# The forget gate's cumulated sums, read from DRAM into all partitions and added by VectorE with the mask, in place of a fourth score product on TensorE

## The chip, the core and the metric

The kernel runs on one core of one Trainium2 chip. A core has TensorE (PE in the profile; PEld is its loading of weights), VectorE (DVE), ScalarE (ACT), GpSimd (POOL) and SyncE (SP), each with its own instruction queue worked in order, and 16 DMA engines that all queues share. Nearly all transfers here are issued from SP. The metric is the device time of one execution in microseconds; the kernel before takes 613.34 us (median of three runs, 612.76 to 614.09).

## The reference

A decoder block over 528 tokens (16 learned ones and 512 real ones), model width 1024, float32. From `u = rmsnorm(h)` one wide projection gives the inputs of two attentions with 16 heads each, and all gates. The MLA branch ("latent" below) has rotary scores of its own; the forgetting attention (FoX, "forget" below) adds differences of cumulated log forget gates to its scores:

```python
log_f = jax.nn.log_sigmoid((f_logit + fox_forget_b[l]).astype(jnp.float32)).transpose(0, 2, 1)
cum = jnp.cumsum(log_f, axis=-1)
...
s = jnp.einsum('bhqd,bhkd->bhqk', qb, k, preferred_element_type=jnp.float32) * scale
if cq is not None:
    s = s + (cq[..., :, None] - cum[:, :, None, :])
s = jnp.where(key_pos[None, :] <= qpos[:, None], s, -jnp.inf)
p = jax.nn.softmax(s, axis=-1)
return jnp.einsum('bhqk,bhkd->bhqd', p.astype(v.dtype), v)
```

The two branch outputs are gated, projected, summed, projected again and normalized onto the residual stream. In a softmax over keys the term `cq` of the query is the same for a whole row and falls out, so the kernel adds only `-cum` of the key.

## The kernel before

Weights and activations are split into a high and a low part, and a product is made of three matmuls (high by high, high by low, low by high). ScalarE casts the high part of a weight tile (`wh`, L142), GpSimd or VectorE subtracts for the low one (`wl`, L118).

**Order of the work.** An opening normalizes the tokens, makes the small projections and the gate's sums; its instruction order is written by hand in three lists (`OPENING`, `MIDDLE`, `LAST`) for all engines. Then come 16 attention passes, two heads each: for each pair of heads 0 to 7 first the forget pass (`br` = 1), then the latent pass (`br` = 0). From the second pass on, TensorE's order is the program's, and a scheduler places the other engines' and SP's instructions by priority and by what they depend on. A last part mixes the branches and projects out.

**A pass** (`attention`): the scores of query blocks 0, 1 and 2 (group 0) fill four PSUM banks (`st`, a pool of four), two for each head; then the value products of the pass before (`values`, tile `ov`); then query block 3 (group 1) fills the four banks again, in two pieces of 272 and 256 keys; then projections of later passes. Both heads' matmuls use 64 rows of the array each and run side by side. For every piece one VectorE instruction (L915) adds the mask, scales, writes `sf` to SBUF and keeps the running minimum `nb`. ScalarE takes the exponential of `sf` with its sum, VectorE inverts the sum (`su`, `ri`), ScalarE and VectorE write the high and low halves of the weights (`pn`, L953 and L954), and eight DMA transposes on SP (L961) turn them into `pt`, which the value products in the next pass read.

**The fourth product.** In a forget pass `sets` gives three products of query and key and a fourth: `ONE`, whose first two rows of each half are ones, by `CT`, which holds the high and low part of `-cum/scale` in those rows. `CT` is filled by `chc` and `chl` for pair 0, and by `load_ct` (L288) from `c_dram` for later pairs. A latent pass has two rotary products in that place. `maskt` (bfloat16) is zero except for one block of 128 columns with -1e30 above the diagonal; a slice of it serves every piece.

`gT[0]` and `gT[1]` hold the gated outputs of the two branches, one slot of 512 columns for a pair of heads; the slots are empty until their pair's value products, and the rotary work of the opening and of the latent pass of pair 1 (`pe_unit`) borrows some of them.

## Time and profile before

| | us |
|---|---|
| profiled execution, its own time | 612.84 |
| its span, first to last instruction | 611.0 |
| median of three runs | 613.34 |
| VectorE busy | 384.7 |
| ScalarE busy | 385.2 |
| GpSimd busy | 174.3 |
| matmuls into `st`, forget and latent, three products of query and key (480) | 47.2 |
| VectorE, score pieces with mask (128) | 48.5 |

Busy times are sums of instruction durations on one engine; matmuls are pipelined, so theirs overlap one another. TensorE's granted clock is full over the whole span (mean 0.999). The DMA engines moved 84.63 MB, and their packets took 53.4% of 16 engines' time.

### The profile page before, as it was taken

What the parts mean: (1) busy time and instruction counts of PE and PEld (TensorE: products, weight loads), DVE (VectorE), ACT (ScalarE), POOL (GpSimd) and SP (SyncE); (2) the same over time, 40 slices, a digit from 0 to 9 for tenths busy, and PEclk for the clock granted to TensorE, in tenths of its full rate; (3) what the DMA queues carried; (4) which work ended last, traced back from release to release, by engine and by line L of the source; (5) the groups of instructions that cost most, each with busy time, mean ns of one, the idle gap of its engine ahead of it and who ended that gap; (6) DMA issues with size and microseconds to landing.
All of it is one profiled execution on the core that took longest, in us unless ns stands there. A gap on an engine that the chain in (4) does not pass through costs nothing.

```text
span 611.0 us, 11593 instructions
## 1 busy us (share of the span) xinstructions
PE 602.2 (99%) x4066; PEld 493.3 (81%) x4066; DVE 384.7 (63%) x1026; ACT 385.2 (63%) x839; POOL 174.3 (29%) x231
## 2 busy tenths in 40 slices
PE   9999999999999999999999999999999999999995
PEld 5889779889889889889888898878888865565885
DVE  5949664774774774773675665668877765646133
ACT  6856884874874884784785766768667743534421
POOL 2002562436543444253343532500000000004600
PEclk9999999999999999999999999999999999999999
DMA  9613577768577477567556665758341146342202
GB/s 301 137 35 109 151 144 182 150 166 206 135 173 183 99 162 156 133 151 167 133 132 159 143 144 145 171 119 240 99 144 36 35 122 228 97 135 77 99 34 105
DMA packets 204556, 84.63 MB, mean 138 GB/s; under 512 B 122757, under 2 KB 197893, under 8 KB 204498
## 3 DMA queue, kind: packets, MB, share of 16 engines
q1 hardware_dynamic: 204496, 83.89, 53.4%
q8 instruction: 32, 0.52, 0.4%
q14 instruction: 26, 0.21, 0.1%
q10 hardware_dynamic: 2, 0.00, 0.0%
HBM read 54.43 MB, written 4.00 MB: 96 GB/s over the span
## 4 chain that ended last, share of the span: by engine, by line
PE 88%; DMA 3%; DVE 2%; issue 2%; ACT 2%; POOL 1%; SPq 0%; DVEq 0%; POOLq 0%; ACTq 0%
PE pg L92 14%; PE z L92 13%; PE st L92 8%; PE v L92 8%; PE po L92 7%; PE fq L92 7%; PE fk L92 7%; PE py L92 6%; PE ov L92 5%; PE yx L92 3%; PE psm L92 2%; PE yy L92 2%; PE mq L92 2%; PE vt L95 1%; DMA ht<-in_x_dram 1%
## 5 line engine op out<-in xcount | busy, mean ns | idle before, releaser
L118 POOL TENSOR_TENSOR wl<-wraw,wh 128x1024 fp32r<-128x1024 f32 (+1 forms) x54 | 119.5, 2218 | 256.1 <-ACT wh L142 246.5
L142 ACT CAST wh<-wraw 128x1024 fp32r<-128x1024 f32 (+1 forms) x74 | 72.9, 986 | 81.2 <-issue 34.4
L925 ACT ACTIVATE sf<-sf,nb 128x144 f32<-128x144 f32 (+3 forms) x128 | 71.9, 566 | 2.8 <-DVE nb L915 2.8
L953 ACT ACTIVATE pn<-sf,ri 128x128 f16<-128x128 f32 (+3 forms) x128 | 61.9, 552 | 16.3 <-ACT sf L925 14.4
L954 DVE SCALAR_TENSOR_TENSOR pn<-sf,ri,pn 128x128 f16<-128x128 f32 (+3 forms) x128 | 66.2, 558 | 8.4 <-ACT pn L953 8.4
L92 PE MATMUL pg<-uTh,wh 128*128 128x512 f32 x128 | 51.9, 406 | 0.0
L915 DVE CUSTOM_DVE_ANT_0 sf<-st,maskt 128x272 f32<-128x272 f32 (+2 forms) x128 | 48.5, 435 | 4.4 <-PE st L92 4.4
L92 PE MATMUL z<-uTh,wh 128*128 128x512 f32 x128 | 51.1, 399 | 0.0
L92 PE MATMUL z<-uTh,wl 128*128 128x512 f32 x128 | 50.1, 391 | 0.0
L92 PE MATMUL z<-uTl,wh 128*128 128x512 f32 x128 | 50.1, 391 | 0.0
L92 PE MATMUL pg<-uTh,wl 128*128 128x512 f32 x128 | 50.0, 391 | 0.0
L92 PE MATMUL pg<-uTl,wh 128*128 128x512 f32 x128 | 49.9, 389 | 0.0
L92 PE MATMUL st<-hlk,hlq 64*128 64x272 f32 (+3 forms) x480 | 47.2, 306 | 0.0
L92 PE MATMUL py<-g,yw 128*128 128x512 f16 x192 | 42.6, 379 | 0.6 <-DVE yw L1239 0.6
L92 PEld LDWEIGHTS st<-hlk,hlq 64*128 64x128 f32 x480 | 35.0, 185 | 5.9 <-ACT wh L142 2.9
L92 PE MATMUL fk<-uTh,wh 128*128 128x256 f32 (+1 forms) x128 | 36.6, 286 | 0.0
L92 PE MATMUL v<-uTh,wh 128*128 128x256 f32 (+1 forms) x128 | 36.5, 285 | 0.0
L92 PE MATMUL fk<-uTl,wh 128*128 128x256 f32 (+1 forms) x128 | 36.5, 285 | 0.0
L92 PE MATMUL fk<-uTh,wl 128*128 128x256 f32 (+1 forms) x128 | 36.5, 285 | 0.0
L92 PE MATMUL v<-uTl,wh 128*128 128x256 f32 (+1 forms) x128 | 36.4, 285 | 0.0
L92 PE MATMUL v<-uTh,wl 128*128 128x256 f32 (+1 forms) x128 | 36.4, 285 | 0.0
L92 PEld LDWEIGHTS <-yw 128*128 128x128 f16 x192 | 17.9, 98 | 22.7 <-DVE yw L1239 1.1
(301 smaller groups left out, 1494.2 us busy)
## 6 DMA issues: line engine op xcount, KB each, us to landing
wraw<-in_w_in_dram SPq DMA_DIRECT2D x56, 512.0 KB
yraw<-in_w_br_fox_dram SPq DMA_DIRECT2D x8, 512.0 KB
yraw<-in_w_br_mla_dram SPq DMA_DIRECT2D x8, 512.0 KB
wraw<-in_w_out_dram SPq DMA_DIRECT2D x8, 512.0 KB
pt<-pn SPq DMA_TRANSPOSE x128
xr<-in_x_dram SPq DMA_DIRECT2D x4, 512.0 KB
out_dram<-yo SPq DMA_DIRECT2D x8, 256.0 KB
QP<-qpe_dram SPq DMA_DIRECT2D x7, 256.0 KB
```

The lines of the kernel that those rows point to most:

```text
L92: nc.tensor.matmul(*a, **k)
L95: nc.tensor.transpose(*a)
L118: eng.tensor_tensor(out=lo, in0=src, in1=f32(hi), op=ALU.subtract)
L142: nc.scalar.copy(wh[:, :n], raw[:, :n])
L915: nc.vector.tensor_tensor_reduce(out=sf_of(h, b)[:, c0 : c0 + w], in0=ps[h][:, o : o + w], in1=maskt[:, m0 : m0 + w], scale=-scale, scalar ...
L925: nc.scalar.activation(sf, sf, AF.Exp, bias=sums["nb"][:, h, b : b + 1], scale=-1.0, accum_out=sums["su"][:, h, b : b + 1])
L953: nc.scalar.activation(hi, sf, AF.Copy, scale=rib)
L954: nc.vector.scalar_tensor_tensor(out=lo, in0=sf, scalar=rib, in1=hi, op0=ALU.mult, op1=ALU.subtract)
```

## The change

The fourth product goes. `c_dram` keeps `-cum/scale` in float32 (no split), one row for each head. For a pair of heads, four DMAs read the two heads' rows into all 128 partitions: `load_diag` puts the whole row of 528 into `cdiag`, `load_off` puts the first 400 into the last slot of `gT[0]` and `gT[1]`. The mask's triangle is added to the four diagonal blocks of `cdiag` in one instruction over 128 x 1024 (`mask_diag`), by VectorE for pair 0 and by GpSimd for the others. The VectorE instruction that empties a score piece then takes its addend from one of these tiles in place of `maskt`; where a piece holds keys both before and in the diagonal block, it becomes two instructions. To make room, `junk` moves and some borrowed slots of `gT` are others; the second half of the rotary table for `pe_unit(1)` is loaded by a DMA of its own.

```diff
-    CT = fx.tile([128, L], F32R, tag="CT", name="CT")
-    ONE = fx.tile([128, 128], F32R, tag="ONE", name="ONE")
...
+    cdiag = fx.tile([128, 2, L], F32, tag="cdiag", name="cdiag")
...
-    def load_ct(pr):
+    OFF = META + 384
+
+    def load_diag(pr):
         for h in range(2):
-            nc.sync.dma_start(f32(CT[64 * h : 64 * h + 2, :]), c_dram[:, 2 * pr + h, :])
+            nc.sync.dma_start(cdiag[:, h], c_dram[2 * pr + h : 2 * pr + h + 1, :].broadcast_to([128, L]))
+
+    def load_off(pr):
+        for h in range(2):
+            nc.sync.dma_start(gT[h][:, KD - 1, 0:OFF],
+                              c_dram[2 * pr + h : 2 * pr + h + 1, 0:OFF].broadcast_to([128, OFF]))
+
+    def mask_diag(eng):
+        d = cdiag[:, :, META:].rearrange("p h (b c) -> p h b c", b=4)
+        m = maskt[:, 400:L].unsqueeze(1).unsqueeze(1).broadcast_to([128, 2, 4, 128])
+        eng.tensor_tensor(out=d, in0=d, in1=m, op=ALU.add)
...
             if pr > 1 and i:
-                load_ct(pr)
+                load_diag(pr)
+                load_off(pr)
+                mask_diag(nc.gpsimd)
...
     def chc():
-        nc.scalar.activation(ch[:, 0], fa[:, 0], AF.Copy, scale=-1.0 / SC_FOX)
-        for h in range(2):
-            nc.sync.dma_start(f32(CT[64 * h : 64 * h + 1, :]), f32(ch[h : h + 1, 0]))
+        nc.scalar.activation(ch, fa[:, 0], AF.Copy, scale=-1.0 / SC_FOX)
+        nc.sync.dma_start(c_dram, ch)
 
     def chl():
-        nc.vector.scalar_tensor_tensor(out=ch[:, 1], in0=fa[:, 0], scalar=-1.0 / SC_FOX, in1=f32(ch[:, 0]),
-                                       op0=ALU.mult, op1=ALU.subtract)
...
+        load_diag(0)
...
     LAST = (
-        "r1 r0 wlm pg2 pg3 pg4 pg5 pg6 pg7 th whb Lf"
+        "Lo bt r1 r0 wlm pg2 pg3 pg4 pg5 pg6 pg7 th whb Lf"
     ).split()
...
             def srcs():
-                nc.sync.dma_start(rp, rope_pe)
+                for cs in range(2):
+                    nc.sync.dma_start(rp[cs], rope_pe[:, cs])
...
                 if br:
-                    return out + [(ONE[hs], CT[hs, ks])]
+                    return out
...
+            def terms(h, b, c0, w):
+                if not br:
+                    m0 = 384 - 128 * b + c0
+                    return [(c0, w, maskt[:, m0 : m0 + w])]
+                d, e = META + 128 * b if b else 0, c0 + w
+                out = [(c0, min(d, e) - c0, gT[h][:, KD - 1, c0 : min(d, e)])] if c0 < d else []
+                return out + ([(d, e - d, cdiag[:, h, d:e])] if e > d else [])
...
-                                    mm(ps[h][:, o : o + w], Q, K, start=(i == 0), stop=(i == 4 - br))
+                                    mm(ps[h][:, o : o + w], Q, K, start=(i == 0), stop=(i == 4 - 2 * br))
...
+                                for c1, n, add in terms(h, b, c0, w):
+                                    with tc.high_priority(offset=100):
+                                        nc.vector.tensor_tensor_reduce(
+                                            out=sf_of(h, b)[:, c1 : c1 + n], in0=ps[h][:, o + c1 - c0 : o + c1 - c0 + n],
+                                            in1=add, scale=-scale, scalar=3.0e38 if c1 == 0 else nb,
+                                            op0=ALU.add, op1=ALU.min, accum_out=nb)
...
-                    load_ct(1)
+                    load_diag(1)
+                    load_off(1)
```

`Lo` in `LAST` is `load_off(0)`, `bt` is `mask_diag` on VectorE; for pair 1 `mask_diag` on GpSimd stands at the end of the first pass.

The change moves instructions on VectorE and on SP. The first place is VectorE in the forget pass of pair 4: the score pieces of group 0 (`sf_3251`; `st_3252` and `st_3253` are the two heads' first banks, `st_3274` and `st_3275` their second), and what stands behind them. Each piece is followed by a row that writes out `nb`, left out here but for the first. Before:

```order
L915 ISA sf_3251,nb_3248<-st_3252,maskt 128x144
L915 ISA nb_3248 128x1
...
L915 ISA sf_3251,nb_3248<-st_3252,maskt 128x272
...
L915 ISA sf_3251,nb_3248<-st_3253,maskt 128x144
...
L915 ISA sf_3251,nb_3248<-st_3253,maskt 128x272
...
L915 ISA sf_3251,nb_3248<-st_3274,maskt 128x400
...
L915 ISA sf_3251,nb_3248<-st_3275,maskt 128x400
...
L934 TENSOR_SCALAR su_3249<-su_3249 128x2x3
L935 RECIPROCAL ri_3250<-su_3249 128x2x3
L976 SCALAR_TENSOR_TENSOR gT_831<-ov_3292,vsc_2897,sil_2918 128x512
```

The same place in the changed kernel, where `gT_822` and `gT_826` are the two tiles `gT`, `st_3263` and `st_3264` the second banks, and `sf_3309` group 1:

```order
L927 ISA sf_3242,nb_3239<-st_3243,gT_822 128x144
...
L927 ISA sf_3242,nb_3239<-st_3244,cdiag 128x144
...
L927 ISA sf_3242,nb_3239<-st_3243,cdiag,nb_3239 128x128
...
L927 ISA sf_3242,nb_3239<-st_3264,gT_826 128x272
...
L927 ISA sf_3242,nb_3239<-st_3263,cdiag,nb_3239 128x128
L927 ISA nb_3239 128x1
L988 SCALAR_TENSOR_TENSOR gT_822<-ov_3281,vsc_2885,sil_2906 128x512
...
L927 ISA sf_3309,nb_3239<-st_3310,gT_822 128x272
...
L927 ISA sf_3309,nb_3239<-st_3321,cdiag,nb_3239 128x128
...
L946 TENSOR_SCALAR su_3240<-su_3240 128x2x3
```

Group 0 has ten pieces where it had six, group 1 six where it had four, and `su`, `ri` and with them `pn` now stand behind all sixteen instead of between the groups.

The second place is SP in the same pass, with its transposes (`pt_...` is the tile of one head). Before:

```order
L133 DMA wraw_2859<-in_w_in_dram 128x8x128
L961 DMA_TRANSPOSE pt_629<-pn_627 128x3x128
L288 DMA CT<-c_dram 2x528
L961 DMA_TRANSPOSE pt_630<-pn_627 128x3x128
L288 DMA CT<-c_dram 2x528
L961 DMA_TRANSPOSE pt_629<-pn_627 128x5x128
```

And in the changed kernel:

```order
L132 DMA wraw_2847<-in_w_in_dram 128x8x128
L289 DMA gT_822<-c_dram 128x400
L289 DMA gT_826<-c_dram 128x400
L285 DMA cdiag<-c_dram 128x528 x2
L973 DMA_TRANSPOSE pt_624<-pn_622 128x3x128
L973 DMA_TRANSPOSE pt_625<-pn_622 128x3x128
```

The loads for the next pair stand ahead of all eight transposes; they wait until VectorE has read the tiles for the last time in this pass.

The third place is SP from the end of the first forget pass to the transposes of the latent pass of pair 0. Before:

```order
L961 DMA_TRANSPOSE pt_630<-pn_628 128x9x128
L288 DMA CT<-c_dram 2x528 x2
L781 DMA qpe_dram<-gT_831 6x16x512 x4
...
L961 DMA_TRANSPOSE pt_629<-pn_627 128x7x128
L961 DMA_TRANSPOSE pt_630<-pn_627 128x7x128
L961 DMA_TRANSPOSE pt_629<-pn_628 128x9x128
```

And in the changed kernel:

```order
L973 DMA_TRANSPOSE pt_625<-pn_623 128x9x128
L285 DMA cdiag<-c_dram 128x528 x2
L289 DMA gT_822<-c_dram 128x400
L289 DMA gT_826<-c_dram 128x400
L786 DMA qpe_dram<-gT_822 6x16x512 x4
...
L973 DMA_TRANSPOSE pt_625<-pn_622 128x7x128
L751 DMA gT_822<-in_rope_pe_dram 128x512
L973 DMA_TRANSPOSE pt_624<-pn_623 128x9x128
```

Four broadcast loads stand where two small ones did, and the second half of the rotary table is loaded between the transposes, since its slot of `gT[0]` is free only after the stores to `qpe_dram`.

More of the change, by code (lines that the diff above doesn't have):

```diff
@@ L80, in block_kernel @@
     nc.gpsimd.memset(ALL1, 1.0)
-    junk = const.tile([128, 1024], BF16, tag="junk", name="junk")
     padp = ctx.enter_context(tc.tile_pool(name="padp", bufs=1, side="right"))
     padp.tile([128, 56], F32, tag="pad", name="pad")
-    c_dram = dram.tile([2, NH, L], F32, tag="cdram", name="c_dram")
+    c_dram = dram.tile([NH, L], F32, tag="cdram", name="c_dram")
     qpe_dram = dram.tile([NH, 2, 2, 16, S], F32, tag="qpedram", name="qpe_dram")
@@ L95, in tps, with sumsq @@
         nc.tensor.transpose(*a)
-    def sumsq(src, acc):
+    def sumsq(src, acc, junk):
         with nc.allow_low_precision(reason="a bound for a power of two"):
@@ L396, in chc @@
     def chc():
-        nc.scalar.activation(ch[:, 0], fa[:, 0], AF.Copy, scale=-1.0 / SC_FOX)
-        for h in range(2):
-            nc.sync.dma_start(f32(CT[64 * h : 64 * h + 1, :]), f32(ch[h : h + 1, 0]))
+        nc.scalar.activation(ch, fa[:, 0], AF.Copy, scale=-1.0 / SC_FOX)
+        nc.sync.dma_start(c_dram, ch)
     def chl():
-        nc.vector.scalar_tensor_tensor(out=ch[:, 1], in0=fa[:, 0], scalar=-1.0 / SC_FOX, in1=f32(ch[:, 0]),
-                                       op0=ALU.mult, op1=ALU.subtract)
-        for h in range(2):
-            nc.sync.dma_start(f32(CT[64 * h + 1 : 64 * h + 2, :]), f32(ch[h : h + 1, 1]))
-        for i in range(2):
-            nc.sync.dma_start(c_dram[i], f32(ch[:, i]))
+        load_diag(0)
     later.update(ab=ab, ex=ex, lnf=lnf, st=st_, scan=scan, chc=chc, chl=chl)
@@ L732, in pe_unit @@
         def pe_unit(g, get0=None, put=None):
-            tt, rp = (gT[1][:, 2:6], gT[1][:, 6:8]) if g else (tt0, rope0_t)
+            tt = gT[1][:, 2:6] if g else tt0
+            rp = (gT[1][:, 6], gT[0][:, 2]) if g else [rope0_t[:, i] for i in range(2)]
             def rr(*sl):
-                return gT[0][:, 4 * g : 4 * g + 4].bitcast(F32R)[sl]
+                return gT[0][:, 3 * g : 3 * g + 4].bitcast(F32R)[sl]
             out = []
@@ L1041, in block_kernel @@
                 [128, KD, S], F32, tag=f"gT{b}", name=f"gT{b}") for b in range(2)]
-            later.update(r1=lambda: rope0[1](1), r0=lambda: rope0[1](0), Lf=fills[1][0][1].load)
+            later.update(r1=lambda: rope0[1](1), r0=lambda: rope0[1](0), Lf=fills[1][0][1].load,
+                         Lo=lambda: load_off(0), bt=lambda: mask_diag(nc.vector))
             for name in LAST:
@@ L1115, in block_kernel @@
         s1x = ExitStack()
+        junk = scp.tile([128, 1024], BF16, tag="junk", name="junk", bufs=1)
         aop = s1x.enter_context(tc.tile_pool(name="aop", bufs=4))
@@ L1225, in square @@
             def square(self, _):
-                sumsq(self.raw, self.ss[:, 0:1])
+                sumsq(self.raw, self.ss[:, 0:1], junk)
             def scale(self):
```

21 lines of the change are left out of this document (7 added, 14 removed).

## The prediction, written before the run

> **What bounds the kernel now.** I read the page first, then what TensorE waited for, then the chain of waits.
>
> ```profile
> span 611.0 us, 11593 instructions
> PE 602.2 (99%) x4066; PEld 493.3 (81%) x4066; DVE 384.7 (63%) x1026; ACT 385.2 (63%) x839; POOL 174.3 (29%) x231
> PE 88%; DMA 3%; DVE 2%; issue 2%; ACT 2%; POOL 1%; SPq 0%; DVEq 0%; POOLq 0%; ACTq 0%
> ```
>
> TensorE runs for 99% of the span and makes up 88% of the chain that ended last; the other engines sit at 63% or less. The second view says whether TensorE ever waits inside the attention (engine, line, what it waited for, us in total, times, longest):
>
> ```profile
> PE v L92 <- DVE hlk L118: 0.4, 1, 0.4
> PE ov L92 <- DMA pt<-pn: 0.3, 1, 0.3
> ```
>
> Only 0.7 us, both early. So a TensorE instruction that goes is time that goes, and whatever makes TensorE wait anew is time that comes. The two questions are what the fourth product costs on TensorE, and whether its replacement stays hidden. The chain of waits shows one forget pass (pair 4) and the latent pass behind it (start us, us, what):
>
> ```profile
> 240.33 1.88 PE st L92 x24
> 242.21 1.97 PE ov L92 x26
> 244.18 1.17 PE st L92 x16
> ...
> 260.11 2.29 PE st L92 x29
> ...
> 264.37 1.42 PE st L92 x13
> ```
>
> A pass is two groups of scores with the previous pass's value products (`ov`) between them. The forget pass has four products, the latent pass five of the same widths.
>
> **What goes: the fourth product.**
>
> ```profile
> L92 PE MATMUL st<-CT,ONE x80: 269/282/343, 64.8 to 375.3; 64*128 64x272 f32 x32, 64*128 64x144 f32 x16, 64*128 64x400 f32 x16, 64*128 64x256 f32 x16
> ```
>
> All 80 go. Their own durations overlap (both heads run side by side), so I take the difference of the passes: one product costs 2.29 - 1.88 = 0.41 us in the first group and 1.42 - 1.17 = 0.25 us in the second. That is 0.66 us a pass and **-5.28 us** over eight. Two small DMA issues a pass, VectorE's `chl` and the memsets of `CT` and `ONE` go as well; TensorE waits for none of them, so they count nothing.
>
> **What VectorE gets.** VectorE empties the score banks of pair 4 like this (start us, us, instruction):
>
> ```profile
> 241.61 0.31 DVE L915 CUSTOM_DVE_ANT_0 sf<-st,maskt 128x144 f32<-128x144 f32 x1
> 241.84 0.44 DVE L915 CUSTOM_DVE_ANT_0 sf<-st,maskt 128x272 f32<-128x272 f32 x1
> ...
> 242.79 0.57 DVE L915 CUSTOM_DVE_ANT_0 sf<-st,maskt 128x400 f32<-128x400 f32 x1
> 243.29 0.57 DVE L915 CUSTOM_DVE_ANT_0 sf<-st,maskt 128x400 f32<-128x400 f32 x1
> ...
> 245.87 0.71 DVE L976 SCALAR_TENSOR_TENSOR gT<-ov,vsc,sil 128x512 f32<-128x512 f32 x1
> ...
> 247.83 0.47 DVE L915 CUSTOM_DVE_ANT_0 sf<-st,maskt,nb 128x256 f32<-128x256 f32 x1
> 248.24 0.47 DVE L915 CUSTOM_DVE_ANT_0 sf<-st,maskt,nb 128x256 f32<-128x256 f32 x1
> 248.64 1.93 DVE L954 SCALAR_TENSOR_TENSOR pn<-sf,ri,pn 128x256 f16<-128x256 f32 x4
> ```
>
> From start to start, 144 columns take 0.23, 272 take 0.36, 400 take 0.50, and 256 with the running minimum `nb` as input 0.41. The slope is 0.27/256 us a column, so a piece of 128 with `nb` takes about 0.41 - 0.13 = 0.28. Before, the first group is 2 x (0.23 + 0.36 + 0.50) = 2.18 us; after, 2 x (0.23 + 0.23 + 0.28 + 0.36 + 0.28) = 2.76 us. That the added operand is now float32 rather than bfloat16 isn't shown for this instruction; the row at 248.64 reads float32 from SBUF alone at 0.46 us for 256 columns, close to the 0.41 here, so I take no extra cost. The upper bound, double time per column, is a rival below.
>
> The banks matter because there are four, and the second group needs all of them again (TensorE, start us, us):
>
> ```profile
> 244.11 0.64 PE L92 MATMUL st<-hlk,hlq 64*128 64x272 f32 x6
> 244.58 0.29 PE L92 MATMUL st<-CT,ONE 64*128 64x272 f32 x2
> 244.71 0.51 PE L92 MATMUL st<-hlk,hlq 64*128 64x256 f32 x6
> ...
> 262.33 0.41 PE L92 MATMUL ov<-pt,vm 80*64 80x512 f16 x2
> ```
>
> The second group's second bank starts at 244.71. Without the product it would start 0.41 + 0.13 earlier, at 244.17. VectorE, starting at 241.61 as before (the `v` scale ahead of it is unchanged), ends at 241.61 + 2.76 + 0.08 (an instruction's end lies that far behind the next one's start) = 244.45. Before it ended at 243.86, 0.85 us in time; now it is **0.28 us late**. Pairs 2 to 7 have the same offsets within 0.02 us: **+1.7 us**. Pair 0 has projections between its groups and pair 1 is late for another reason, so both are left out. Bounds: 0, if the first evacuations overlap better, to 0.6 a pass.
>
> [...]
>
> **The transposes.** The order moves VectorE's `su`, `ri` and `pn` behind all score pieces, and SP's four broadcast loads ahead of the eight transposes, where two small loads lay among them.
>
> ```profile
> 247.41 1.18 SPq L961 DMA_TRANSPOSE pt<-pn  x1
> 248.69 0.39 SPq L288 DMA_DIRECT2D CT<-c_dram  x1
> ...
> 250.93 8.01 SPq L961 DMA_TRANSPOSE pt<-pn  x6
> ```
>
> ```profile
> 248.45 0.72 ACT L925 ACTIVATE sf<-sf,nb 128x528 f32<-128x528 f32 x1
> ```
>
> After: score pieces of group one end at 244.37, `gT` takes 0.62 to the next start, group two 2 x (0.36 + 0.28 + 0.28) = 1.84, so 246.83; two exponentials of 0.72 to 248.3; the first `pn` pair about 0.4 on each engine, so the first transpose starts near 249.1 and not at 247.41. The loads wait for group two's last read of their tiles (246.8 at most) and take four issues of some 0.43 (the row at 45.82 below, also 128 rows): done at 248.5, just hidden. The eight transposes need 258.94 - 247.41 less two `CT` loads with gaps of 0.48, 10.6 us: they end at 259.7, the last one issued at 258.4. TensorE wants it at 262.33 - 0.66 + 0.28 = 261.95, 3.6 us later. How long does one take to land?
>
> ```profile
> 81.84 4.11 DMA pt<-pn
> ```
>
> ```profile
> 397.75 10.65 SPq L961 DMA_TRANSPOSE pt<-pn  x8
> ```
>
> ```profile
> 409.00:409.50 0.50, 0.50 (x4) 0.41 (x3) 0.50 (x1) 0.27 (x1) 0.00 (x0) 1.00 1.05 232
> 409.50:410.00 0.50, 0.50 (x4) 0.40 (x3) 0.50 (x1) 0.00 (x0) 0.00 (x0) 1.00 0.00 0
> ```
>
> Once, in the opening, 4.11 us. At the end of attention, with no load behind it, the last issue began at 408.40 - 1.33 = 407.07 and the DMA engines (last two columns: share, GB/s) fell silent by 409.5: 2.4 us. Inside the passes I take 2.4 to 3.3: **0** here, with a margin of 0.3 to 1.2 us.
>
> In the opening there is no margin:
>
> ```profile
> 83.26 0.76 SPq L288 DMA_DIRECT2D CT<-c_dram  x2
> 84.08 3.91 SPq L781 DMA_DIRECT2D qpe_dram<-gT  x4
> ...
> 95.05 3.15 SPq L961 DMA_TRANSPOSE pt<-pn  x2
> ...
> 98.91 8.73 SPq L961 DMA_TRANSPOSE pt<-pn  x6
> ```
>
> ```profile
> 45.82 0.43 SPq L746 DMA_DIRECT2D gT<-in_rope_pe_dram  x1
> ```
>
> ```profile
> 109.16 0.51 PE L92 MATMUL ov<-pt,vm 80*64 80x512 f16 x2
> ```
>
> SP is busy without a gap from 83.26 to 107.64, and the last transpose, issued at 107.64 - 1.46 = 106.18, is wanted at 109.16. After, four loads of 0.43 with gaps of 0.09 replace 0.76 (+1.3), and half of the `rope_pe` load now lies among the transposes (+0.4): issued at 107.9, landed 2.4 later at 110.3. TensorE would have been there at 109.16 - 0.66 - 0.41 = 108.1, so **+2.2 us**. Bounds: 0, if SP was held up there by what it waited for rather than by issuing, to 3.9 with 4.11 to land.
>
> **Edits at nothing.** The mask added by GpSimd costs about what this does:
>
> ```profile
> 253.29 2.40 POOL L118 TENSOR_TENSOR wl<-wraw,wh 128x1024 fp32r<-128x1024 f32 x1 [1.43 <-ACT wh L142]
> ```
>
> It lands ahead of such a row, in idle time (GpSimd is at 29%), some 15 us ahead of the next forget pass; without that cover it would cost up to 2.4 a pass. Writing `c_dram` and reading it back for pair 0, and VectorE's mask there (1.2), have this cover:
>
> ```profile
> 65.62 0.31 DVE L915 CUSTOM_DVE_ANT_0 sf<-st,maskt 128x144 f32<-128x144 f32 x1 [4.21 <-PE st L92]
> ```
>
> VectorE sat idle for 4.21 us there; past that, each further us is one of the total. The moved `junk` and rotary tiles hold the same instructions. The loads bring about 0.95 MB a pass; they sit in front of the transposes, and only delay them if they are not through in 10 us.
>
> **The sum.** -5.28 + 1.7 + 2.2 = -1.4 us. The profiled execution took 612.84 us for its span of 611.0, and lies 0.5 under the median of the runs shown, 613.34. So 611.4 against its own time and **611.9** as a median; I forecast 611.9, its own range 610.3 to 613.3.
>
> [...]
>
> **The rivals.**
> - *Nearly the full saving.* The opening's SP time was waiting, not issuing, and hides the loads; only the evacuation wait remains, or not even that. For it: TensorE waited 0.3 us for a transpose in all of before. Time 613.34 - 5.28 + 0 to 1.7 = 608.1 to 609.8. Chance 0.25.
> - *Late transposes in every pass (slower).* Place: `ov` of the latent pass, pairs 1 to 6. It decides from the point where a transpose takes over 3.6 us to land, or the first starts after 249.1. With 4.11 us it costs 0.5 x 6 and more with the loads' data ahead of it; with issues of 0.98 us (as the four at 84.08) the loads end at 250.8, 1.7 us past 249.1, and TensorE waits 1.7 - 0.3 and more, six times. Time 614.6 to 621. Against it: those stores at 84.08 write to DRAM, the loads do not. Chance 0.20.
> - *Float32 addends at half speed, or a mask that comes late.* The 816 columns of two heads would take 1.7 us more in the first group, six or seven times: 622. Chance 0.08.
> - *The forecast.* Chance 0.47.
>
> **How the numbers follow.** A measurement of this kernel can tell about 0.2%, 1.2 us, from no change, so faster means under 612.1. The forecast puts 0.25 there and 0.22 within; the first rival is all faster; of the last two 0.22 is slower and 0.06 within. Faster 0.50, same 0.28, slower 0.22. The range leaves out the best half of the first rival and the worst of the last two: 608.6 to 615.5.
>
> **What would show it.** TensorE's `st` groups should last 1.47 and, with a wait for VectorE's `sf` of about 0.3, 1.2 us in pairs 2 to 7; the waits of TensorE should list `st <- DVE sf` with some 1.7 us and `ov <- DMA pt` with some 2 us in two places. If `ov <- DMA pt` shows six or more times, the slower rival holds. If no `st` wait shows, the 0.28 is wrong; if the pieces of 128 take over 0.5 us, the float32 rival holds.

## The result, and the profile after

The changed kernel is slower: **619.50 us** (median of 4 runs, 617.81 to 620.40) against 613.05 for the kernel before, a ratio of 1.010, 95% interval 1.0072 to 1.0128. The forecast was 611.9 with a range to 615.5. The profiled execution took 620.40 us for a span of 618.4, so it lies 0.9 above its median; before, 612.84 for 611.0. One execution of the kernel best3 below took 1514.82 us, far from its other five (615.59 to 619.08), and is left out of its median.

From the page after, the span, the engines and the shares by engine of the chain of work that ended last:

```profile
span 618.4 us, 11603 instructions
PE 601.8 (97%) x3986; PEld 490.4 (79%) x3986; DVE 400.9 (65%) x1122; ACT 384.0 (62%) x839; POOL 192.9 (31%) x234
PE 41%; DVE 2%; issue 0%; DMA 0%; ACT 0%; DVEq 0%; ACTq 0%
```

The shares of the chain add up to 43% of the span, so it was followed back only that far, and the 41% can't be set beside the 88% of before. TensorE has 80 matmuls fewer, yet its busy time is only 0.4 us shorter, and the span is 7.4 longer. Its waits (engine, line, what it waited for, us in total, times, longest) name three new ones; before, the first had 0.3 us and the other two weren't there:

```profile
PE ov L91 <- DMA pt<-pn: 3.5, 4, 2.1
PE mk L91 <- DVE hlq L117: 2.5, 3, 1.1
PE vt L94 <- DVE nb L927: 1.8, 2, 1.0
```

Since every pass begins with TensorE's first `st`, the time can be followed pass by pass. The table holds the profiled executions of six kernels, worked out from the timeline of TensorE: us from one pass's first `st` to the next one's. The four kernels in the middle are experiments below. F is a forget, L a latent pass, the number is the pair; the last column ends with the first matmul that mixes the branches (at 437.26 before, 445.10 after).

| kernel | F0+L0+F1 | L1 | F2 to F7 | L2 to L6 | L7 to the mixing | sum |
|---|---|---|---|---|---|---|
| before | 62.69 | 26.40 | 118.69 | 118.08 | 47.03 | 372.89 |
| before without the product | 62.54 | 26.39 | 113.68 | 118.54 | 47.67 | 368.82 |
| after, no loads, earlier transposes | 63.43 | 26.40 | 117.45 | 118.09 | 47.33 | 372.70 |
| after, no loads | 63.66 | 26.40 | 116.00 | 119.41 | 48.30 | 373.77 |
| after, no mask | 67.20 | 26.39 | 116.02 | 121.46 | 47.51 | 378.58 |
| after | 67.54 | 26.40 | 119.61 | 119.48 | 47.90 | 380.93 |

So 4.85 of the 8.04 us came in the opening, 0.92 in six forget passes that should have become shorter, and 2.27 in the latent passes.

**The opening.** TensorE's timeline at the first latent values (start us, us, instruction, what it waited for), and three windows around it (stretch, us, busy time and instructions of PE, PEld, DVE, ACT and POOL, granted clock, DMA share, GB/s):

```profile
108.22 1.52 PE L91 MATMUL st<-hlk,hlq 64*128 64x144 f32 x18
...
111.83 0.38 PE L91 MATMUL ov<-pt,vm 80*64 80x512 f16 x1 [2.09 <-DMA pt<-pn]
112.93 0.58 PE L91 MATMUL ov<-pt,vm 80*64 80x512 f16 x1 [0.72 <-DMA pt<-pn]
```

```profile
109.70:111.80 2.10, 0.04 (x2) 0.07 (x1) 2.10 (x17) 2.10 (x9) 2.10 (x2) 1.00 1.24 236
111.80:115.30 3.50, 2.74 (x15) 1.55 (x16) 0.57 (x6) 1.68 (x6) 0.11 (x1) 0.56 1.03 281
115.30:118.80 3.50, 3.50 (x34) 3.00 (x31) 2.51 (x14) 0.09 (x1) 0.00 (x0) 0.95 0.98 129
```

TensorE waits 2.09 us, works for one matmul and waits 0.72; meanwhile its clock falls. In steps of half a microsecond the granted clock is 0.71 in the one from 112.0, 0.50 in all six from 112.5 to 115.5, 0.88 in the next and 1.00 from 116.0 on. The second window was granted 0.56 of the clock and the third 0.95, which is half the clock for 2 x (0.44 + 0.05) x 3.5 = 3.4 us. Work done at half clock for that long loses up to 3.4 x 0.5 = 1.7 us more (an estimate from these figures). SP's queue shows why the transposes are late (start us, us, instruction):

```profile
83.82 1.05 SPq L285 DMA_DIRECT2D cdiag<-c_dram  x2
84.92 0.91 SPq L289 DMA_DIRECT2D gT<-c_dram  x2
85.86 4.26 SPq L786 DMA_DIRECT2D qpe_dram<-gT  x4
...
107.36 0.57 SPq L751 DMA_DIRECT2D gT<-in_rope_pe_dram  x1
108.03 3.01 SPq L973 DMA_TRANSPOSE pt<-pn  x2
```

The four loads take 2.0 us ahead of the `qpe_dram` stores and the moved rotary load 0.6 ahead of the last two transposes, which are issued from 108.03 to 111.0. The value product that waits for the last of them starts at 112.93.

**A forget pass with the mask beside it.** VectorE and GpSimd in pair 4 (two timelines, columns as above; in brackets the wait ahead of it):

```profile
258.49 2.70 DVE L966 SCALAR_TENSOR_TENSOR pn<-sf,ri,pn 128x512 f16<-128x512 f32 x1
261.11 0.68 DVE L117 TENSOR_TENSOR hlq<-mq,hlq 128x512 fp32r<-128x512 f32 x1
```

```profile
258.49 2.15 POOL L295 TENSOR_TENSOR cdiag<-cdiag,maskt 128x1024 f32<-128x1024 f32 x1 [3.34 <-DMA cdiag<-c_dram]
```

The mask starts the moment its load lands. VectorE's `pn`, which reads two tensors from SBUF, starts with it and takes 2.70 us, which is the mask's 2.15 and 0.55 more. The `hlq` behind it comes late, and `mk` of TensorE waits for `hlq` (the second row of the waits). In pair 5 an instruction that reads PSUM (`z`) lay beside the mask, and in pair 7, which has no next pair to mask for, the same `pn` lay alone (VectorE and GpSimd of pair 5, then VectorE of pair 7):

```profile
301.67 0.68 DVE L873 SCALAR_TENSOR_TENSOR sil<-sil,z 128x512 f32<-128x512 f32 x1
```

```profile
301.69 2.16 POOL L295 TENSOR_TENSOR cdiag<-cdiag,maskt 128x1024 f32<-128x1024 f32 x1 [1.73 <-DMA cdiag<-c_dram]
```

```profile
391.20 0.75 DVE L966 SCALAR_TENSOR_TENSOR pn<-sf,ri,pn 128x512 f16<-128x512 f32 x1
```

Neither is held up: `sil` took 0.68 us beside the mask and `pn` 0.75 without one, where `pn` beside the mask took 2.70.

**The latent passes.** The groups of transposes on SP, before and then after (issue time in ns, minimum, median and maximum; first and last start), and two pieces of SP's timeline after, for the forget passes of pairs 4 and 5:

```profile
L961 SPq DMA_TRANSPOSE pt<-pn x128: 1178/1247/2317, 71.1 to 407.1; - x128
```

```profile
L973 SPq DMA_TRANSPOSE pt<-pn x128: 1178/1237/3137, 71.8 to 415.4; - x128
```

```profile
254.07 12.92 SPq L973 DMA_TRANSPOSE pt<-pn  x8
...
298.87 10.62 SPq L973 DMA_TRANSPOSE pt<-pn  x8
```

Most issues take 1.2 us, but single ones take two or three: pair 4's eight took 12.92 us with one of 3.1, pair 5's 10.62 with none. Both kernels have such cases. Before, they had room: the first of pair 4 started at 247.41, 7.1 us into the pass. After, the first starts 8.8 to 8.9 us into it.

A stretched issue isn't the whole of it. In pair 5 all eight were steady and the last was issued at about 308.2, yet a value product of the latent pass waited for its transposed weights until 312.39, and that pass took 24.41 us instead of 23.6:

```profile
312.39 0.38 PE L91 MATMUL ov<-pt,vm 80*64 80x512 f16 x1 [0.41 <-DMA pt<-pn]
```

So here 4.2 us went by from the issue of a transpose to the start of the product that waited for it. From issue to landing the transposes of the whole kernel took 2.3 to 5.5 us, 2.8 at the median.

### The profile page after: what moved, and what is told of

It reads as the page before. It is cut to its first block, busy times and chain, and to the rows that moved or that the text cites. A ratio compares the mean times of both kernels' runs of the same rounds, so it can differ in the third digit from the quotient of the medians.

```text
span 618.4 us, 11603 instructions
## 1 busy us (share of the span) xinstructions
PE 601.8 (97%) x3986; PEld 490.4 (79%) x3986; DVE 400.9 (65%) x1122; ACT 384.0 (62%) x839; POOL 192.9 (31%) x234
## 5 line engine op out<-in xcount | busy, mean ns | idle before, releaser
L117 POOL TENSOR_TENSOR wl<-wraw,wh 128x1024 fp32r<-128x1024 f32 (+1 forms) x54 | 121.0, 2245 | 239.9 <-ACT wh L141 226.0
L937 ACT ACTIVATE sf<-sf,nb 128x272 f32<-128x272 f32 (+3 forms) x128 | 72.0, 567 | 16.7 <-DVE nb L927 16.6
L966 DVE SCALAR_TENSOR_TENSOR pn<-sf,ri,pn 128x128 f16<-128x128 f32 (+3 forms) x128 | 74.1, 619 | 2.9 <-ACT pn L965 2.5
L807 DVE TENSOR_REDUCE vsc<-v 128x1 f32<-128x272 f32 (+1 forms) x32 | 13.2, 432 | 36.5 <-PE v L91 36.5
```

Source lines behind the costliest of these rows:

```text
L117: eng.tensor_tensor(out=lo, in0=src, in1=f32(hi), op=ALU.subtract)
L807: nc.vector.tensor_reduce(out=st["sc"][:, i : i + 1], in_=ps, op=ALU.max, axis=AX.X, apply_absolute_value=True)
L937: nc.scalar.activation(sf, sf, AF.Exp, bias=sums["nb"][:, h, b : b + 1], scale=-1.0, accum_out=sums["su"][:, h, b : b + 1])
L966: nc.vector.scalar_tensor_tensor(out=lo, in0=sf, scalar=rib, in1=hi, op0=ALU.mult, op1=ALU.subtract)
```

## The experiments

The theories are these. **M**, the mask on GpSimd holds up VectorE and is the main loss. **S**, the late start of the transposes leaves them too little room on SP. **Loads**, the broadcast loads cost SP and the DMA engines time, most in the opening. Where a kernel leaves part of the computation out, its expectation says which. Medians in us, ratios to the kernel before on the same chip.

| kernel | edit | median | ratio, 95% |
|---|---|---|---|
| after | | 619.50 | 1.0072 to 1.0128 |
| no_mask | no mask by GpSimd | 619.16 | 1.0077 to 1.0108 |
| late_mask | mask later | 620.75 | 1.0109 to 1.0139 |
| no_load | neither mask nor loads, pairs 1 to 7 | 613.47 | 0.9989 to 1.0016 |
| early_no_load | the same, transposes earlier | 612.38 | 0.9974 to 0.9995 |
| product_out | before less the product | 611.45 | 0.9963 to 0.9989 |
| product_out2 | and less the `CT` loads | 607.25 | 0.9880 to 0.9913 |
| product_back | after, with a fourth product | 638.58 | 1.0391 to 1.0423 |
| early_pn | `pn` ahead of group 1's pieces | 639.49 | 1.0388 to 1.0460 |
| open_act | pair 1's loads on ScalarE | 619.82 | 1.0066 to 1.0125 |
| both | early_pn and open_act | 638.75 | 1.0385 to 1.0436 |
| open2 | pair 1's loads on ScalarE, earlier | 617.33 | 1.0047 to 1.0080 |
| loop_fix | order and loads of the loop | 635.71 | 1.0350 to 1.0397 |
| best | loop_fix and open2 | 635.18 | 1.0324 to 1.0374 |
| loop_fix2 | loop_fix, other engine | 621.71 | 1.0126 to 1.0155 |
| best2 | loop_fix2 and open2 | 619.17 | 1.0079 to 1.0110 |
| best3 | best2, all loads wait | 617.02 | 1.0039 to 1.0078 |

### Is it the mask?

```diff
                 load_off(pr)
-                mask_diag(nc.gpsimd)
...
                     nxt[2].make()
-                    mask_diag(nc.gpsimd)
```

> The changed kernel without GpSimd's mask addition for pairs 1 to 7 (seven instructions of 2.15 us; the diagonal blocks of these pairs stay unmasked); loads, pieces and the order of all engines are the changed kernel's. Theory M (while GpSimd adds the mask, VectorE's subtractions for pn, whose two operands both lie in SBUF, stand still: 2.70 instead of 0.72 us in the forget pass of pair 4, 2.06 instead of 0.78 for two in the latent pass of pair 0): the waits of mk for hlq go (-2.5), vt's wait in the latent pass of pair 0 (-1.0) and most of the 2.8 us wait of ov in the forget pass of pair 1 with its 3.4 us at half clock (-2 to -4): 612.5 to 615. Theory T (the loads on SP's queue make the transposes late) and theory E (the pieces, and VectorE's order with group 1's pieces ahead of pn, make them late): pn is not what waits, 618 to 619.5.

No: 619.16, 0.3 under the changed kernel. The waits for `hlq` go, and others come. The only row of its waits that concerns `ov`:

```profile
PE ov L91 <- DMA pt<-pn: 5.7, 6, 2.7
```

The table by passes shows the exchange: F2 to F7 fall from 119.61 to 116.02, 19.34 each where the forecast had 19.40 for an undisturbed pass, and L2 to L6 rise from 119.48 to 121.46. The `mk` wait had given the transposes time: pair 4's forget pass falls from 20.75 to 19.33 us, and its latent pass rises from 24.05 to 25.62. How much of the total the mask makes up isn't settled: 0.3 us by medians, 2.4 by the two profiled executions' sums; in either case most of the loss stays.

The second try makes the mask wait for the end of the last `hlk` product, by an instruction on one element of `cdiag`:

```diff
+            if pr > 0 and i:
+                one = cdiag[:, 0, META : META + 1]
+                nc.vector.scalar_tensor_tensor(out=one, in0=f32(hls["k", 1, pr][:, 1, L - 1 : L]), scalar=0.0,
+                                               in1=one, op0=ALU.mult, op1=ALU.add)
                 mask_diag(nc.gpsimd)
...
                     nxt[2].make()
-                    mask_diag(nc.gpsimd)
```

> The whole change, with the same seven mask additions on GpSimd, but each made to wait for the last hlk half of the next pair (an addition of 0 times an element of hlk to one element of cdiag, on VectorE), so that it runs while VectorE has no pn to subtract. Loads stay where they are. Theory M: as fast as the kernel without mask within 1 us (612.5 to 615), no pn over 0.8 us. If GpSimd's 2.15 us themselves are the trouble (its splits come late), or the loads, or the order: 618 to 620.

620.75, with the `mk` waits gone and seven `ov` waits of 7.3 us in all. M falls as the main cause.

### Without the loads, and with earlier transposes

```diff
-                load_diag(pr)
-                load_off(pr)
-                mask_diag(nc.gpsimd)
...
-                    load_diag(1)
-                    load_off(1)
...
-                    mask_diag(nc.gpsimd)
```

> As the kernel without mask, and without the four broadcast loads of pairs 1 to 7 too (all forget passes add pair 0's gate rows); the half load of rope_pe moves ahead of the transposes in the opening. What is left of the change is the product gone and the evacuation in pieces. Theory T: the four loads of each pair (1.7 us of issue on SP ahead of the eight transposes, 0.95 MB) are worth 3 us or more against the kernel without mask, and no ov waits for pt. Theories M and E: within 1 us of the kernel without mask, and ov waits in the latent passes of pairs 5 and 7 stay (0.7 us each).

613.47: the loads of pairs 1 to 7 are worth 5.7 us (619.16 less 613.47). By the table it is 4.8 in the profiled executions: 3.5 in the opening (67.20 to 63.66, all of it in F1: 24.16 to 20.62), where the half clock goes too, 2.1 in L2 to L6, and 0.8 the other way in L7. The 3.5 includes that the moved rotary load now stands ahead of the latent pass's transposes and not among them. In the loop the loads don't shift the first transpose, which starts 8.9 us into the pass with and without them. Their 2.1 us lie in one place, the latent pass of pair 4 (25.62 to 23.63): one issue of its eight took 3.3 us with the loads and 1.2 without. Whether their traffic does that isn't shown. The window of F1, whole and at full clock, and what `ov` still waits for:

```profile
107.55:128.17 20.62, 19.36 (x128) 15.65 (x127) 15.51 (x62) 14.86 (x37) 7.62 (x12) 1.00 0.75 155
```

```profile
PE ov L91 <- DMA pt<-pn: 1.5, 2, 1.0
PE ov L91 <- issue: 1.1, 2, 0.9
```

Here transposes are late in places with no load near them. That is for S. The next kernel, again without loads and mask, also puts `su`, `ri` and `pn` of group 0 ahead of group 1's score pieces in the forget passes, where they stood before the change; `big` is a tile of one column that makes the first piece of group 1 wait for `ri`, and the pieces of group 1 lose their raised priority:

```diff
-                                            in1=add, scale=-scale, scalar=3.0e38 if c1 == 0 else nb,
+                                            in1=add, scale=-scale,
+                                            scalar=nb if c1 else (sums["big"] if br and g else 3.0e38),
...
-                                    with tc.high_priority(offset=100):
+                                    with tc.high_priority(offset=0 if br and g else 100):
...
+                    if br and g == 0:
+                        nc.vector.tensor_scalar(out=sums["big"], in0=ri[:, 0, 0:1], scalar1=0.0, scalar2=3.0e38,
+                                                op0=ALU.mult, op1=ALU.add)
...
+                    if br:
+                        n0()
...
-                    n0()
+                    if not br:
+                        n0()
```

> The kernel without loads and mask for pairs 1 to 7 (no_load, 613.5 us), with su, ri and pn of group 0 moved back ahead of group 1's evacuation. One edit against no_load: only the start of the transposes moves, 8.9 to about 7.1 us into the forget pass. Theory S (the late start is what makes ov wait in the loop where no load is about: 2.6 us in the latent passes of pairs 2, 5 and 7 of no_load): these waits go to under 0.5 together, 610.5 to 611.8. If the stretched issues come whatever the start, or ov waits for something else: 612.8 to 614, waits of 1.5 us or more.

612.38. TensorE waits for no transpose in pairs 2 to 7, and L2 to L6 and L7 together fall by 2.3 us to within 0.3 of before: S is shown for these waits. The price is that F2 to F7 rise by 1.45, so only 1.1 us remain, and the two intervals overlap a little. The late order was thus no oversight to be had back for nothing: it shortens the emptying of group 1, and lengthens the way to the transposes.

### The product alone

```diff
-                    return out + [(ONE[hs], CT[hs, ks])]
+                    return out
...
-                                    mm(ps[h][:, o : o + w], Q, K, start=(i == 0), stop=(i == 4 - br))
+                                    mm(ps[h][:, o : o + w], Q, K, start=(i == 0), stop=(i == 4 - 2 * br))
```

> The kernel before with its fourth product left out and nothing put in its place (the gate's sums are missing from the scores; CT is still loaded). This is the whole gain that the change can reach. VectorE's order moves as in the changed kernel: su, ri and pn of group 0 come behind the evacuation of group 1. By the prediction's own sum (0.66 us a pass) 607.8. By what the changed kernel's undisturbed passes show (0.43 at group 0, nothing at group 1, nothing in the opening pass where vt waits for VectorE) 609.5 to 611. Theory E, as far as the new order alone makes the transposes late: 612 to 614, with ov waiting for pt in latent passes.

611.45, but this run doesn't answer: the `CT` loads, which nothing read any more, moved in among the opening's transposes and made pair 1's passes 3.6 us longer. SP there:

```profile
105.14 0.43 SPq L288 DMA_DIRECT2D CT<-c_dram  x1
...
109.38 3.70 SPq L288 DMA_DIRECT2D CT<-c_dram  x4
```

The second form leaves these loads out too (`load_ct` isn't called).

> The kernel before without its fourth product and without CT's loads for pairs 1 to 7 (the gate's sums are missing from the scores). In product_out these loads had lost their readers and twelve of them stood in SP's queue at 105 to 117 us, where the passes of pair 1 took 3.6 us longer than before. So this is the gain that the product alone has in it: if the product is worth 0.83 us in each of the forget passes of pairs 1 to 7, as it was in pairs 2 to 7 of product_out, and nothing in that of pair 0, and no ov waits: 607 to 608.5. If the late start of pn by itself (7.9 us into the pass) or the opening takes it back: 609.5 to 611.5.

**607.25**, 6.0 us under the kernel before: the product was worth a little more than the 5.28 predicted. F1 to F7 shorten by 0.83 each, not 0.66, and F0 by only 0.06: it is bound by VectorE's score pieces there (`vt` waits 0.4 us for `nb`). The two groups of scores give 0.68 of it, as forecast; the other 0.15 is at `mk`, which took 0.89 us of the pass and takes 0.74. Group 1 without the product and with the old pieces lasts 0.92 us (pair 6):

```profile
327.42 0.99 PE L92 MATMUL st<-hlk,hlq 64*128 64x272 f32 x12
328.34 0.50 PE L92 MATMUL z<-uTh,wh 128*128 128x512 f32 x1
```

From here to early_no_load (612.38), which does the product's work in VectorE but has no load and no mask after pair 0, is +5.1 us by the medians and 3.88 by the table, of which 3.77 lie in F2 to F7 (0.63 a pass). The scheduler gave product_out2 the late order too, with `su` and `ri` behind group 1. So no_load differs from it in the loop only by the pieces and what they read, and its F2 to F7 are 2.32 longer (0.39 a pass); the early order adds 0.24 a pass. The added pieces thus give back about half of the product's 0.83 us a pass by themselves, and three quarters in the order that doesn't delay the transposes. They delay the transposes too: the first starts 7.2 us into the forget pass before, 7.9 in product_out2 and 8.9 in no_load, so of the 1.75 us about 1.0 come from the pieces and 0.8 from the order.

```diff
-                    return out
+                    return out + [(q[hs, 1, qs], k[hs, 1, ks])]
```

> The whole change, and a fourth product in the forget scores again (the low parts of q and k, 64 rows as the one that was removed; the scores get a term of the size of rounding). It asks what the removal is worth inside the changed kernel. VectorE's order stays late (group 1's evacuation ahead of pn). If the transposes are the bound from group 0's pn to ov, the longer forget pass gives ov's waits back and the removal is worth little: 620 to 622.5 against 619.5. If TensorE's own time is the bound: 0.83 us a pass as in the run with the product left out, 624 to 626.

Both expectations missed. With a fourth product put back into the changed kernel (and `stop` set for four), the mask on GpSimd and the `wl` behind it fell beside VectorE's work in the latent passes, and TensorE's `vt` waited for VectorE's pieces eight times:

```profile
PE vt L94 <- DVE nb L927: 15.2, 8, 2.9
```

So 638.58 is the time of another order and says nothing about the product.

### Mending the loop

The kernels of this section, and those that add the opening to them, try to have the early order with the loads. The first keeps everything else and has `big` as above:

```diff
+                    if br:
+                        n0.first()
```

> The whole change, but with su, ri and pn of group 0 ahead of group 1's evacuation in the forget passes of pairs 1 to 7, as in the kernel before (group 1's first pieces read their start value 3.0e38 from a tile that is worked out from ri). Of the loads, cdiag's two move behind the sixth and seventh transpose. Theory S (the eight transposes leave SP one after the other in 10.5 us; in the changed kernel they start 1.75 us later in the pass, at 8.9 instead of 7.15, which uses up the 1.8 us between the last landing and ov in the next pass, so that each stretched issue becomes a wait): first transpose at 7.2 to 7.6, ov's waits in the latent passes of pairs 2 to 7 (2.2 us) gone to under 0.5, mk's waits for hlq (2.7 us) gone too as pn is done before the mask starts; the opening as it was: 614 to 615.5. Theory T (the loads and their traffic, wherever pn stands): ov's waits of 1.5 us or more stay, 617 to 619.5.

639.49, against what S expected. The first transpose started 8.5 us into the pass, not the 7.2 to 7.6 expected, and still before the tiles `cdiag` were free, so the `cdiag` loads fell behind six or seven of the transposes. GpSimd's mask stood first in its queue, waiting, with the `wl` of the next weights behind it, and VectorE then met that `wl` in its own `pn`. GpSimd, then VectorE:

```profile
278.39 2.13 POOL L295 TENSOR_TENSOR cdiag<-cdiag,maskt 128x1024 f32<-128x1024 f32 x1 [6.64 <-DMA cdiag<-c_dram]
282.97 2.39 POOL L117 TENSOR_TENSOR wl<-wraw,wh 128x1024 fp32r<-128x1024 f32 x1
285.30 0.41 POOL L964 TENSOR_TENSOR mt<-sf,ri 128x96 f32<-128x96 f32 x1
```

```profile
283.10 2.76 DVE L978 SCALAR_TENSOR_TENSOR pn<-sf,ri,pn 128x128 f16<-128x128 f32 x2
```

The latent passes' transposes then start 11.4 us and more into the pass, and `ov` waits 15.0 us in eight places.

> The whole change, loops rearranged: in the forget passes su, ri and pn of group 0 ahead of group 1's evacuation, as in the kernel before; cdiag's two loads wait for the end of the forget pass (a small read of cdiag with vsc as factor), so that none stands among its eight transposes; the mask waits for the last hlk half of the next pair. The opening's loads stay in SP's queue. Theory S+M (in the loop what costs is the transposes' late start and GpSimd's mask beside pn, or GpSimd's queue standing behind a mask that waits for its load; not the loads as such): first transpose at 7.2 to 7.9 in the pass, no wait of mk, ov's waits in the latent passes of pairs 2 to 7 under 0.7 us together, the forget pass of pair 1 as bad as before or worse: 614 to 616. Theory T (the loads as such): ov's waits of 1.5 us or more in these latent passes, 617 to 620.

Here the `cdiag` loads wait for the end of the forget pass by a small read `dep` on VectorE. 635.71: the read waited 2.42 us for a scale from GpSimd and stood beside a `wl`, in each latent pass (26.6 us instead of 23.6):

```profile
276.87 2.30 DVE L305 TENSOR_SCALAR dep<-cdiag,vsc 128x2 f32<-128x2 f32 x1 [2.42 <-POOL vsc L828]
```

A VectorE instruction over 256 numbers thus took 2.30 us.

> As loop_fix, but the small read of cdiag that cdiag's loads wait for is made by ScalarE behind vT. In loop_fix VectorE made it: it waited 2.4 us for GpSimd's vsc and then took 2.30 us beside GpSimd's split, in every latent pass. Theory S+M: no such stall, forget passes of 19.3 to 19.6 us with the first transpose at 7.1 to 7.9, latent passes of pairs 2 to 6 of 23.6 to 23.9 without waits of ov; the opening's forget pass of pair 1 as before or worse: 614 to 616.5. Theory T (the loads as such make the transposes late): waits of ov of 1.5 us or more in the latent passes of pairs 2 to 7, 617 to 620.

With `dep` on ScalarE the latent passes take 23.6 to 25.1 us, but the `gT` loads, which did not wait for `dep`, now stood between the transposes: 621.71.

```profile
306.18 1.00 SPq L289 DMA_DIRECT2D gT<-c_dram  x2
307.35 3.37 SPq L992 DMA_TRANSPOSE pt<-pn  x2
```

### Mending the opening

```diff
-                    load_diag(1)
-                    load_off(1)
...
+                    load_diag(1, nc.scalar)
+                    load_off(1, nc.scalar)
```

> The whole change, but the four loads for pair 1 in the opening are issued by ScalarE's queue instead of SP's, at the end of the first forget pass. Theory O (in the opening SP's queue is the bound: the four loads and the half load of rope_pe stand ahead of the latent pass's transposes, and the wait that they make is over 2 us, after which TensorE runs 3.4 us at half clock): the wait of ov in the forget pass of pair 1 falls from 2.8 to under 1.5 us, the half clock goes, that pass takes 20 to 21.5 us instead of 23.5; 615.5 to 617. If the traffic of the loads, and not their place in SP's queue, is what counts: that pass stays over 22.5 us and the time at 618 to 620.

F1 becomes 19.35 us, as short as the later forget passes. But the total is 619.82, since the loads on ScalarE's queue stopped ScalarE itself, behind a store that they had to wait for:

```profile
89.85 0.42 ACT L937 ACTIVATE sf<-sf,nb 128x144 f32<-128x144 f32 x1 [3.91 <-DMA qpe_dram<-gT]
```

L0 became 28.89 us, 4.2 longer. L0 and F1 together took 48.24 us, 48.17 in the changed kernel: the transposes had the time that the latent pass lost, so this run by itself doesn't show that F1's loss came from SP's queue.

> The two edits together (pn of group 0 early; pair 1's loads on ScalarE's queue). By theories S and O their gains add: 610.5 to 612, just faster than the kernel before. By theory T 616 or more.

638.75: early_pn's loss again, and L0 26.92 us.

> The whole change, but pair 1's four loads in the opening issued by ScalarE's queue ahead of the last two pn of the first forget pass, where the transfers whose counters they wait for are earlier ones than in the first try (there the third load stood 3.9 us behind qpe_dram's write, with group 0's exponentials behind it). Theory O (SP's queue is the bound in the opening): the forget pass of pair 1 in 19.5 to 21.5 us in place of 23.5, no half clock there, the latent pass of pair 0 no longer than in the changed kernel: 614.5 to 617. If the loads hold ScalarE up again, or their traffic counts: 618.5 to 621.

The same loads, issued on ScalarE ahead of `pn` of group 1: 617.33. F1 takes 20.78 at full clock (0.999 granted on the mean of the whole span), but F0 20.78 and L0 25.03, so 1.8 of the 2.7 us won in F1 go back in the two passes ahead of it. Here, and in no_load (44.24), L0 and F1 together are shorter: 45.82 us for 48.17. Both fit a loss that came from the loads' place in SP's queue, though their place on ScalarE cost F0 and L0 most of it again.

### Both together

> Both rearrangements together, the whole computation. If the causes named (late start of the transposes, GpSimd's mask beside pn, SP's queue in the opening) are all: 609.5 to 612, 0.2 to 0.6% under the kernel before. If a part of the loss comes from the loads as such: 613 or more.

635.18: `dep` on VectorE again.

> loop_fix2 and open2 together, the whole computation. From the passes seen so far: the opening to the end of pair 1's forget pass 64.7 us (run best; 67.5 in the changed kernel, 62.7 before), pairs 1 to 7 without waits 308.3 us up to the merge, the merge as before: span 610.5, 611.5 to 613.5 us in all, so no difference from the kernel before to 0.2%. If waits of ov stay: 615 or more.

619.17: L0 took 27.82, at a lowered clock for a part (from 82 to 108 us 0.93 was granted on the mean), and the loop still waited as loop_fix2 did.

> best2 with the two gT loads too waiting for the end of the forget pass: in best2 they stood between the sixth and seventh transpose, the issues of the last two took 1.3 to 2.6 us and they landed 3.6 to 6.0 us later, and ov waited 0.5 to 1.7 us in four latent passes. If loads cost only where they stand among the transposes, ov waits under 0.7 us in the latent passes of pairs 2 to 7 and the time is 612 to 615, by how the opening falls out (64.7 to 66.9 us to the end of pair 1's forget pass in the two runs so far). If their traffic at the start of the latent pass makes that pass's own transposes late: waits of ov in forget passes, 616 or more.

With the `gT` loads waiting as well, 617.02. From 170 us to 440 us TensorE has one wait, and none for a transpose:

```profile
PE mk L91 <- DVE hlq L117: 1.0, 1, 1.0
```

Still 1.0059 times the kernel before: F0, L0 and F1 take 65.23 us (62.69 before), and L2 to L6 119.19 (118.08). What these passes lose now wasn't followed further. No version with the whole computation was faster than the kernel before.

## Why the prediction was wrong

Three terms of the sum failed: the opening at +2.2, the mask at nothing and the transposes inside the passes at 0. Against the sum the table is 4.0 us worse in the opening, 3.2 in F2 to F7 and 2.3 in L2 to L7. The two terms worked out from VectorE's and TensorE's own rows came out nearly right.

- **The product, -5.28: right, and 0.7 small.** Alone it gives -6.0.
- **The emptying, +0.28 a pass: right in its place, small in size.** VectorE's first group after, pair 4:

```profile
246.47 0.31 DVE L927 CUSTOM_DVE_ANT_0 sf<-st,cdiag 128x144 f32<-128x144 f32 x1
...
247.38 0.35 DVE L927 CUSTOM_DVE_ANT_0 sf<-st,cdiag,nb 128x128 f32<-128x128 f32 x1
...
247.65 0.35 DVE L927 CUSTOM_DVE_ANT_0 sf<-st,cdiag,nb 128x128 f32<-128x128 f32 x1
...
249.19 0.75 DVE L988 SCALAR_TENSOR_TENSOR gT<-ov,vsc,sil 128x512 f32<-128x512 f32 x1
```

  Its ten pieces take 2.72 us (246.47 to 249.19), where 2.76 was worked out, and those of 128 columns 0.27 from start to start. Pieces of 272 columns take 435 ns with the float32 `gT` and 432 with the bfloat16 `maskt` (means of 32 each, after). So the float32 addends cost nothing more than the bfloat16 ones, and the rival that had them at half speed falls. TensorE after, pair 6:

```profile
333.70 1.52 PE L91 MATMUL st<-hlk,hlq 64*128 64x144 f32 x18
335.15 0.41 PE L91 MATMUL ov<-pt,vm 80*64 80x512 f16 x2
337.12 1.36 PE L91 MATMUL st<-hlk,hlq 64*128 64x272 f32 x12
338.41 0.50 PE L91 MATMUL z<-uTh,wh 128*128 128x512 f32 x1
```

  From 337.12 to 338.41 are 1.29 us, where product_out2 has 0.92, so the wait is 0.37 a pass. It is inside the group and the list of waits has no row for it; by the prediction's own sign, that no `st` wait shows, the 0.28 would have been called wrong, so the sign was at fault. An undisturbed forget pass came out at 19.33 or 19.34 us, where 19.78 - 0.66 + 0.28 is 19.40. What the sum left out is F0: there the product's going saves almost nothing (0.06 us in product_out2), and TensorE's `vt` waited 1.0 us for the pieces (F0 18.60 to 19.38).
- **The transposes inside the passes, 0: failed.** Much of its working held: the first was to start at 249.1, 8.8 us into the pass, and did at 8.9; the last one is issued after some 18.2 us, where 18.1 was worked out; it lands 2.3 to 2.9 us later when nothing is near; TensorE wants it 21.6 us into the pass. What failed is to take steady issues for all eight and a landing of at most 3.3 us, and to call 0.3 to 1.2 us a margin. The row of before already held an issue of 2317 ns against a median of 1247, 1.07 us more: by itself as much as the whole margin. And in pair 5 the product that waited for a transpose started 4.2 us after its issue. Before, the last of pair 4 was issued 17.4 us into the pass and wanted at 22.1, which leaves 1.8 us past a landing of 2.9 (measured after); after, by the same count, 0.5. The slower rival had this place, and its first condition (over 3.6 us to land) was met in pairs 4 and 5 (up to 5.5 and some 4.2), but it asked for late landings or late loads in every pass; a few late ones were enough. That the total lies in its price, 614.6 to 621, is luck: most of the loss came from other places. no_load shows these waits without a load, early_no_load shows them gone.
- **The opening, +2.2: right in mechanism and place, half in size.** The last transpose was issued at about 109.5, where 107.9 was worked out, and the value product that waited for it started some 3.5 us later, where 2.4 was taken for the landing. TensorE waited 2.8 us instead of 2.2, and then lost up to 1.7 at half clock, which no term of the sum had. F1 was to take 19.78 - 0.66 + 2.2 = 21.3 and took 23.49. An idle time of 1.0 us there (no_load) left the clock full: 1.00 was granted over F1.
- **The mask at nothing: wrong as a cost, small as a cause.** The cover named, an idle GpSimd, was there; what was left out is whom GpSimd blocks. `pn` took 2.70 for 0.75 and TensorE waited 2.5 us for what lay behind it; F2 to F7 took 3.6 us more than without the mask, and L0 1.0 (24.67, 23.63). Taking it away gave back 0.3 to 2.4 us in all, since the transposes were next.
- **Loads "only delay them if they are not through in 10 us": wrong.** They landed 4.5 and 4.8 us after their issue (medians), and still the kernel without them is 5.7 us faster. By the table 3.5 of 4.8 us are the opening, whose price the prediction had apart; 2.1 are the one late latent pass of pair 4.

The runs that leave parts out follow one another: taking away the mask gives 0.3 us, the loads 5.7, the late order 1.1, and the pieces, with what little else differs, 5.1, from 619.50 down to 607.25 (medians of different chips, on which the kernel before differs by up to 0.4 us).

Against the forecast of -1.4, by the table: the opening +4.85 for +0.88 (two of the savings and 2.2); F2 to F7 +0.92 for -2.26; L2 to L6 +1.40 for 0; L7 +0.87 for 0. That is +8.04; the first pass starts 0.2 earlier, and the part behind the attention is 0.5 shorter, which makes the span's +7.4. What remains open is why single transposes are issued or land late (no run tells a transfer in flight from the queue itself), and how the 5.1 us between product_out2 and early_no_load divide: the profiled execution of the one was the slowest of its four, that of the other the fastest of its ten, so the table has only 3.9 of them.

## What to carry to other kernels

Work taken off the busiest engine pays only as far as what stands behind it has room: here eight serial issues had some 1.8 us, and the change needed 1.3 of it. Hold such a margin against the maximum in a group's row, not its median. Cutting an emptying into more pieces can cost twice, once where TensorE waits for the bank and once where what comes after the pieces starts later. Before putting work on an idle engine, look at what stands behind it in that queue and whom its instruction can hold up; and when a wait is taken away, read the next one before counting the gain.

## What the runs showed of the hardware

- An idle TensorE of 2.09 us, and of 0.72 one matmul later, was followed by some 3.4 us at half clock (0.50). In best2, whose longest wait was 1.7 us, the stretch from 82 to 108 us was granted 0.93 on the mean; open2, whose longest was 1.7 as well, was granted 0.999 over its span, and 1.0 us in no_load left F1 at 1.00.
- A VectorE instruction with two SBUF operands (`pn`) took 2.70 us beside a GpSimd tensor instruction of 2.15 and 0.75 without one; one that also reads PSUM (`sil`) took 0.68 beside it.
- A single transpose issue on SP, 1.2 us at the median, took up to 3.1 us after the change, in the kernel before up to 2.3.
- A DMA issued on ScalarE's queue held the engine for 3.91 us while it waited for another transfer (open_act).
